# Moving the starting addresses of the matmul operands in a hybrid decoder layer

## The chip, the cores and the metric

The kernel runs on one core of a Trainium2 chip. The metric is the device time of one execution in microseconds. The times of the kernel before come from three executions.

## What is computed

One decoder layer on x of 512 tokens by 2048 features, in float32, and a last norm. A conditioning vector c gives a shift, a scale and a gate for each of the two sub-layers. The first sub-layer runs eight heads of causal stick-breaking attention beside a gated linear recurrence (RG-LRU) and projects both together; the second is an MLP of width 8192 with a squared ReLU.

```python
mod = (silu(c) @ w_ada + b_ada).reshape(B, 6, D)
sh1, sc1, gt1, sh2, sc2, gt2 = mod[:, 0..5]
h = rmsnorm(x, g_norm_mix) * (1 + sc1) + sh1
q, k, v, xr, xg = split(h @ w_in)
o_attn = stick_breaking_attention(q, k, v)
o_lru = rg_lru(causal_depthwise_conv(xr)) * gelu(xg)
x = x + gt1 * (concat(rmsnorm(o_attn), rmsnorm(o_lru)) @ w_out)
h = rmsnorm(x, g_norm_mlp) * (1 + sc2) + sh2
x = x + gt2 * (square(relu(h @ w_mlp_in)) @ w_mlp_out)
return rmsnorm(x, g_norm_final)
```

## The kernel before

**How the products are made.** Features lie on the 128 partitions, tokens along the free axis. Nearly every product is made from two halves of each float32 number: a high part, rounded to the type float32r, and a low part, the difference. Three matmuls then make one product: weights high by operand high, weights high by operand low, weights low by operand high (`mm3`, lines 251 to 256, and by hand at lines 463 to 465 for v and 1092 to 1094 in the MLP). So every matmul reads two buffers of the on-chip memory (SBUF): 128 columns of weights, which a separate instruction loads (PEld in the profile), and 256 or 512 columns of the moving operand. For the product that makes v, the roles are exchanged: there `a` is loaded as weights and `wh`, `wl` move.

**The buffers.** A tile of a name (a "tag") takes one of a few buffers in turn. Those that matmuls read:

- `a`: 64 buffers of 512 columns, the activations and their halves (and, in the first stage, the weights too); `n` and `cb`, small work and the conditioning row; the constants `ones`, `ntri`, `nones_r` of 128 columns each.
- `wr` (weights as loaded), `wh` and `wl` (their halves), 512 columns, up to the MLP. After it the same memory holds `w3` (768 columns) and `w5` (1024).
- `x` and `tt`, 1024 and 1280 columns, for the conditioning weights and for attention. After it the same memory holds `ts`, `raw` and `w4` (1024 columns).

The memory of a partition is filled from both ends. On the left stand the small constants, then `cb`, `n`, `a`, `ga`, then the stage's weights (lines 48 to 57, 79 to 91 and 131 to 138). On the right, downward from the top, stand the other buffers of the stage. `vec` begins at byte 16,512, which is 128 past a multiple of 512; the right side begins at byte 229,344, 480 past one. A tile takes whole units of 32 bytes. The buffers of matmul operands are multiples of 512 bytes long, so one number says where all of a side begin, counted from a multiple of 512 bytes:

| buffers | before |
|---|---|
| `ones`, `ntri`, `nones_r`, `cmask` | 0 |
| `cb`, `n`, `a` | 192 |
| `wr`, `wh`, `wl`; later `w3`, `w5` | 320 |
| `x`, `tt`; later `ts`, `raw`, `w4` | 480 |

**The order of the work.** The first stage (to about 110 us) makes the recurrence's input from `a` by `a` with all eight banks of the accumulator memory, while the conditioning weights stream in through VectorE (`prep1`, lines 370 to 377, and the loop at 409). Then come q, k and v (`qk_group`, `v_group`, `group`), with attention and the recurrence as generators between them (`Lane`, lines 262 to 296, gives each a number of ticks), the gate xg and the output projection (`product`, `half_product`). From about 750 us the MLP runs as a Strassen scheme of seven products of 256 columns for each pair of blocks (`strassen`, lines 1073 to 1098; `operands`, 1043 to 1066). There `operands` splits weights as loaded into `w3`, and sums of them into a high and a low tile that come from four `w4` and one `w5` in turn (`split_tag`, line 81). VectorE forms the sums (L1050, L1057, L1058) and the low halves (L121), ScalarE the high halves. The last 1024 features of the MLP go in plain products, and the last norm ends the kernel.

Small constants: `mods` (96 columns, the six modulation vectors), `gm1` and `gm2` (16, norm gain by scale), `spl`, `nspl`, `spe`, `shb` (8, 8, 8, 16, for the recurrence), `eps`. They are read as scalars of one column.

Of the kernel before, what the change touches and what calls it, by code (L numbers as in the profile page):

```python
# [10 lines left out]
F32 = mybir.dt.float32  # L11
# [5 lines left out]
P = 128  # L17
S = 512
D = 2048
NK = D // P  # L20
HEADS = 8
# [19 lines left out]

URGENT = 150
EVAC = 88

# [17 lines left out]
def hybrid_layer_kernel(  # L64
# [12 lines left out]
):  # L77
    nc = tc.nc
    sp = ctx.enter_context(tc.tile_pool(name="sp", bufs=1))
    region = {side: ctx.enter_context(ExitStack()) for side in ("right", "left")}  # L80
    pools, split_tag = {}, itertools.cycle(["w4"] * 4 + ["w5"])

    def stage(name):
        side, tags = STAGES[name]
        for tag in [t for t, (_, _, s) in pools.items() if s == side]:
            del pools[tag]
        region[side].close()
        pool = region[side].enter_context(tc.tile_pool(name=name, bufs=1, reuse_waits="tile", side=side))
        for tag, bufs in tags.items():
            pools[tag] = pool, bufs, side  # L90
            new(tag)
# [5 lines left out]
    def T(tag, dt=F32, cols=None):  # L97
        return new(next(split_tag) if tag == "w4" else tag, dt, cols)

    def new(tag, dt=F32, cols=None):  # L100
        count[0] += 1
        pool, bufs = (sp, BUFS[tag]) if tag in BUFS else pools[tag][:2]
        return pool.tile([P, cols or COLS[tag]], dt, tag=tag, name=f"{tag}_{count[0]}", bufs=bufs)
# [5 lines left out]
    def const(cols, name, dt=F32):  # L109
        return sp.tile([P, cols], dt, tag=name, name=name)  # L110
# [19 lines left out]

    vec = const(NPK, "vec")
    ones, ntri, nones_r = const(P, "ones"), const(P, "ntri", F32R), const(P, "nones_r", F32R)
    cmask, eps, mods = const(P, "cmask"), const(1, "eps"), const(96, "mods")
    gm1, gm2 = const(NK, "gm1"), const(NK, "gm2")
    spl, nspl, spe, shb = const(HEADS, "spl"), const(HEADS, "nspl"), const(HEADS, "spe"), const(2 * HEADS, "shb")
    cb = [T("cb"), T("cb")]
    stage("rows")
    stage("front")
    nc.scalar.dma_start(vec, pk)
# [122 lines left out]
    class Lane:  # L262
# [8 lines left out]
        def next(self):  # L271
            if not self.queue:
                return False
            try:
                self.wait += next(self.queue[0]) or 0.0
            except StopIteration:
                self.queue.pop(0)
            return True
# [155 lines left out]
    for o in range(8):  # L434
        t = T("a")
# [11 lines left out]
    def qk_evac(bs, h0, os=range(4)):  # L447
        for b in os:
            h, lo = T("a", F32R), T("a", F32R)
            s = QSCALE if b < 2 else 1.0  # L450
            with tc.high_priority(offset=EVAC):
                act(h, bs[b], AF.Copy, scale=s)
# [14 lines left out]
    def v_evac(bs, h0, os=range(4)):  # L467

        for o in os:
            p, b = o // 2, o % 2  # L470
            h, lo = T("a", F32R), T("a", F32R)
            with tc.high_priority(offset=EVAC):
                act(h, bs[o], AF.Copy)
# [140 lines left out]
    def scores(hd):  # L614
# [18 lines left out]
        nh, nl = T("tt", F32R), T("tt", F32R)  # L633
        with tc.high_priority(offset=EVAC):
            act(nh, e, AF.Copy)
# [605 lines left out]
    for i, (n, ps) in enumerate(parts):  # L1241
        seen = {m for m, _ in parts[: i + 1]}
        left = [m for m, _ in parts[i + 1 :]]
# [11 lines left out]
        if n not in left and n < NO - 1:  # L1255
# [10 lines left out]
            with tc.high_priority(offset=SETW):  # L1266
                for k, tok, q in quarters(n, *qs):
                    t = x2[k][:, tok]
# [8 lines left out]
        else:  # L1277
            with tc.high_priority(offset=SETE):
                for j, b in enumerate(bs):
                    t = T("a")  # L1280
# [14 lines left out]
    for p in final:  # L1295
        t = T("a", F32R)
# [156 lines left out]
```

## Time and profile before

| what | value |
|---|---|
| time, median of 3 | 2045.92 us (2044.84 to 2047.92) |
| span of the profiled execution, first to last instruction | 2043.4 us |
| share of the span in the chain that ended last: TensorE | 55% |
| the same: VectorE, DMA, issue | 3%, 1%, 1% |
| DMA moved | 441.45 MB, 216 GB/s mean |

No time of its own besides the span is given for the profiled execution; the span is 2.5 us under the median of the executions without a profile. A matmul in the profile has a start and a duration, but matmuls are pipelined and overlap: of 128x256 ones, 282 ns long by the profile, one starts every 119 ns or so. So the durations say little, and the time between starts is the quantity to read. "MATMUL ps_mm<-a,w 128*128 128x256" is a matmul into a bank of the pool `mm`, with moving operand or weights in `a` and in a tile whose name begins with w.

### The profile page before, as it was taken

How to read it: one execution, taken by the hardware profiler on the slowest of the kernel's cores; microseconds unless marked ns; L12 is line 12 of the kernel's file. 1: busy time of each engine (PE TensorE's matmuls, PEld its weight loads, DVE VectorE, ACT ScalarE, POOL GpSimd, SP SyncE). 2: the span in 40 equal slices, each digit the busy share in tenths (PEclk: the TensorE clock that was granted, in tenths of full speed). 3: DMA queues.
4: the chain of work that ended last, by engine and by line, in shares of the span. 5: the costliest groups of instructions: out<-in, count | busy, mean ns of one | idle time of the engine just before them, and what ended most of it. 6: DMA issues, size and time to landing. Idle time of an engine off the chain costs nothing.

```text
span 2043.4 us, 37927 instructions
## 1 busy us (share of the span) xinstructions
PE 2003.8 (98%) x14532; PEld 1890.2 (93%) x14532; DVE 1764.1 (86%) x2971; ACT 1078.3 (53%) x1572; POOL 180.7 (9%) x283
## 2 busy tenths in 40 slices
PE   8999999999999998999999999999999999999997
PEld 6788898778788998999999999999999999999996
DVE  8998776988898599999999999999778778778986
ACT  5443664796433485655555555456445445545542
POOL 0000000000000001121112112200010110210000
PEclk9999999999999999999999999999999999999998
DMA  9895645556689454676556556655476667667644
GB/s 364 299 326 195 214 150 187 177 171 208 219 277 338 145 153 157 190 231 206 195 194 221 193 174 221 227 190 182 150 281 226 230 237 249 228 242 254 243 149 150
DMA packets 205624, 441.45 MB, mean 216 GB/s; under 512 B 20353, under 2 KB 41985, under 8 KB 205442
## 3 DMA queue, kind: packets, MB, share of 16 engines
q1 hardware_dynamic: 178642, 360.78, 52.9%
q0 software_dynamic: 21760, 71.32, 9.4%
q10 hardware_dynamic: 5040, 6.93, 1.0%
q8 instruction: 114, 1.87, 0.4%
q14 instruction: 68, 0.56, 0.1%
HBM read 375.25 MB, written 63.70 MB: 215 GB/s over the span
## 4 chain that ended last, share of the span: by engine, by line
PE 55%; DVE 3%; DMA 1%; issue 1%; ACT 0%; SPq 0%; DVEq 0%; ACTq 0%
PE ps_mm L1093 9%; PE ps_mm L1094 9%; PE ps_mm L1092 9%; PE ps_z L1093 7%; PE ps_z L1094 7%; PE ps_z L1092 7%; PE ps_o L1094 2%; PE ps_o L1093 2%; PE ps_o L1092 2%; DVE w L121 1%; DMA raw<-in_w_mlp_out_dram 1%; DMA a<-x 0%; DMA a<-sum 0%; DVE a L1269 0%; DVE a L1339 0%
## 5 line engine op out<-in xcount | busy, mean ns | idle before, releaser
L1094 PE MATMUL ps_mm<-a,w 128*128 128x256 f32 x1696 | 477.3, 282 | 1.3 <-DVE w L121 1.3
L1093 PE MATMUL ps_mm<-a,w 128*128 128x256 f32 x1696 | 478.5, 282 | 0.0
L1092 PE MATMUL ps_mm<-a,w 128*128 128x256 f32 x1696 | 474.9, 281 | 0.0
L1056 ACT ACTIVATE w<-raw 128x768 fp32r<-128x768 f32 x244 | 204.9, 841 | 349.5 <-PE ps_mm L1093 158.8
L121 DVE TENSOR_TENSOR w<-ts,w 128x1024 fp32r<-128x1024 f32 x244 | 298.0, 1221 | 101.2 <-PE ps_mm L1093 52.9
L1094 PE MATMUL ps_z<-a,w 128*128 128x256 f32 x1304 | 368.3, 283 | 6.2 <-DVE w L121 6.2
L1093 PE MATMUL ps_z<-a,w 128*128 128x256 f32 x1304 | 368.4, 283 | 0.0
L1092 PE MATMUL ps_z<-a,w 128*128 128x256 f32 x1304 | 366.4, 281 | 0.0
L1062 ACT ACTIVATE w<-ts 128x1024 fp32r<-128x1024 f32 x244 | 258.5, 1059 | 129.5 <-DVE ts L1058 117.4
L1094 PEld LDWEIGHTS ps_mm<-a,w 128*128 128x128 f32 x1696 | 319.3, 188 | 1.6 <-DVE w L121 1.5
L1092 PEld LDWEIGHTS ps_mm<-a,w 128*128 128x128 f32 x1696 | 319.8, 189 | 0.1
L1093 PEld LDWEIGHTS ps_mm<-a,w 128*128 128x128 f32 x1696 | 319.0, 188 | 0.3 <-DVE a L121 0.2
L121 DVE TENSOR_TENSOR w<-raw,w 128x768 fp32r<-128x768 f32 (+1 forms) x296 | 267.3, 904 | 36.8 <-ACT w L237 24.9
L1094 PEld LDWEIGHTS ps_z<-a,w 128*128 128x128 f32 x1304 | 246.2, 189 | 7.3 <-DVE w L121 7.1
L1092 PEld LDWEIGHTS ps_z<-a,w 128*128 128x128 f32 x1304 | 246.6, 189 | 0.2
L1093 PEld LDWEIGHTS ps_z<-a,w 128*128 128x128 f32 x1304 | 245.8, 189 | 0.2
L237 ACT ACTIVATE wh<-wr 128x512 fp32r<-128x512 f32 (+1 forms) x184 | 113.2, 619 | 162.5 <-PE ps_mm L255 67.8
L252 PE MATMUL ps_mm<-a,wh 128*128 128x512 f32 x448 | 178.1, 397 | 1.5 <-DVE a L453 0.9
L256 PE MATMUL ps_mm<-a,wl 128*128 128x512 f32 x448 | 177.6, 396 | 0.5 <-DVE wl L121 0.4
L255 PE MATMUL ps_mm<-a,wh 128*128 128x512 f32 x448 | 176.8, 395 | 0.0
L1050 DVE TENSOR_TENSOR ts<-raw 128x512 f32<-128x512 f32 x244 | 166.6, 684 | 8.0 <-DMA raw<-in_w_mlp_out_dram 7.8
L121 DVE TENSOR_TENSOR wl<-wr,wh 128x512 fp32r<-128x512 f32 (+1 forms) x184 | 123.4, 674 | 35.8 <-ACT wh L237 35.1
(332 smaller groups left out, 4152.2 us busy)
## 6 DMA issues: line engine op xcount, KB each, us to landing
raw<-in_w_mlp_out_dram SPq DMA_DIRECT2D x124, 512.0 KB, 4.2
raw<-in_w_mlp_in_dram SPq DMA_DIRECT2D x120, 512.0 KB, 3.8
x<-in_w_adaT_dram SPq DMA_DIRECT2D x108, 512.0 KB, 5.9
wr<-in_w_in_dram SPq DMA_DIRECT2D x160, 256.0 KB, 3.4
tt<-in_w_adaT_dram SPq DMA_DIRECT2D x52, 512.0 KB, 6.6
part<-a POOLq DMA_DIRECT2D x84, 256.0 KB, 3.7
a<-part SPq DMA_DIRECT2D x84, 256.0 KB, 6.3
prod<-a POOLq DMA_DIRECT2D x63, 256.0 KB, 5.9
```

The lines of the kernel that those rows point to most:

```text
L121: tt(out=out, in0=full, in1=f32(high), op=ALU.subtract)
L237: act(h[:, :n], r[:, :n], AF.Copy)
L252: first = mm(out, wh, ah, start=start, stop=False, **kw)
L255: mm(out, wh, al, start=False, stop=False, **kw)
L256: mm(out, wl, ah, start=False, stop=stop, **kw)
L1050: tt(out=t[:, : 2 * HT].rearrange("p (a b) -> p a b", a=2), in0=r[:, HT : 3 * HT].rearrange("p (a b) -> p a b", a=2), in1=r[:, q_(0)].unsq ...
L1056: act(h, r[:, HT:], AF.Copy)
L1062: act(h, t, AF.Copy)
L1092: mm(out, wh[:, blk(i)], ah, start=st, stop=False, **kw)
L1093: mm(out, wh[:, blk(i)], al, start=False, stop=False, **kw)
L1094: mm(out, wl[:, blk(i)], ah, start=False, stop=j == js[-1], **kw)
```

## The change

The buffers are placed anew; nothing else is edited.

- Three small constants, `mods`, `gm1` and `spl`, move to a pool of their own at the top of the right side, ahead of everything there. They take 384 + 64 + 32 = 480 bytes.
- On the left remain `eps`, `gm2`, `nspl`, `spe` and `shb`, 32 + 64 + 32 + 32 + 64 = 224 bytes, after `cmask`. `ga` (4 buffers of 32 bytes) now follows them, and then a constant `pad` of 40 columns, 160 bytes, that nothing reads or writes.
- `new(...)` is called once for `ga`, `n` and `a` only to fix the order in which the pool places them. The tiles that it makes are not used.
- The stack of pools of the two sides (`region`) is opened after the new pool instead of at the start.

By this arithmetic `cb`, `n`, `a` and the stage's weights begin at 224 + 128 + 160 = 512, a multiple, and so do the buffers of the right side, 480 below a place 480 past one. In the MLP the left side then ends at byte 192,000, where the right side begins.

```diff
+PAD = 40
...
     sp = ctx.enter_context(tc.tile_pool(name="sp", bufs=1))
-    region = {side: ctx.enter_context(ExitStack()) for side in ("right", "left")}
+    region = {}
...
     ones, ntri, nones_r = const(P, "ones"), const(P, "ntri", F32R), const(P, "nones_r", F32R)
-    cmask, eps, mods = const(P, "cmask"), const(1, "eps"), const(96, "mods")
-    gm1, gm2 = const(NK, "gm1"), const(NK, "gm2")
-    spl, nspl, spe, shb = const(HEADS, "spl"), const(HEADS, "nspl"), const(HEADS, "spe"), const(2 * HEADS, "shb")
+    top = ctx.enter_context(tc.tile_pool(name="top", bufs=1, side="right"))
+    cmask, eps, gm2 = const(P, "cmask"), const(1, "eps"), const(NK, "gm2")
+    nspl, spe, shb = const(HEADS, "nspl"), const(HEADS, "spe"), const(2 * HEADS, "shb")
+    mods, gm1, spl = (top.tile([P, n], F32, tag=t, name=t) for n, t in ((96, "mods"), (NK, "gm1"), (HEADS, "spl")))
+    region |= {side: ctx.enter_context(ExitStack()) for side in ("right", "left")}
+    new("ga")
+    const(PAD, "pad")
     cb = [T("cb"), T("cb")]
+    for tag in ("n", "a"):
+        new(tag)
     stage("rows")
     stage("front")
```

## The prediction

> **What bounds the kernel now.** I read the page first, then the table of busy time by stage, then the waits of TensorE, and last the timeline of single matmuls.
>
> ```profile
> span 2043.4 us, 37927 instructions
> PE 2003.8 (98%) x14532; PEld 1890.2 (93%) x14532; DVE 1764.1 (86%) x2971; ACT 1078.3 (53%) x1572; POOL 180.7 (9%) x283
> ```
>
> TensorE is busy for 98% of the span, VectorE for 86%. In the table by stage the columns are the stretch, its length, busy time and instructions of PE, PEld, DVE, ACT and POOL, the granted clock, the DMA share and GB/s:
>
> ```profile
> 0.00:110.00 110.00, 98.00 (x399) 77.32 (x400) 100.08 (x192) 52.22 (x85) 5.25 (x9) 0.98 0.92 335
> 110.00:700.00 590.00, 584.93 (x3101) 497.49 (x3100) 475.55 (x808) 307.00 (x479) 14.46 (x14) 1.00 0.66 218
> 700.00:800.00 100.00, 93.22 (x749) 91.86 (x748) 88.86 (x188) 70.01 (x142) 3.52 (x6) 0.97 0.40 125
> 800.00:1000.00 200.00, 199.35 (x1676) 198.88 (x1674) 196.44 (x340) 108.98 (x145) 37.50 (x55) 1.00 0.66 214
> 1000.00:1400.00 400.00, 399.98 (x3367) 399.55 (x3366) 381.01 (x645) 218.00 (x292) 59.33 (x87) 1.00 0.61 202
> 1400.00:1990.00 590.00, 588.40 (x4944) 587.33 (x4944) 486.30 (x728) 307.13 (x404) 60.62 (x112) 1.00 0.63 224
> 1990.00:2043.40 53.40, 39.96 (x310) 37.76 (x308) 35.83 (x76) 14.98 (x31) 0.00 (x0) 0.90 0.45 147
> ```
>
> From 110 to 1990 us TensorE hardly stops, at the full granted clock. The longest waits of TensorE are these (who waited, for whom: total us, times, longest):
>
> ```profile
> PE ps_mm L252 <- ACT a L375: 7.7, 2, 5.2
> PE ps_z L1094 <- DVE w L121: 6.2, 3, 4.1
> ```
>
> So nothing is to be won by removing waits. The time is the number of matmuls times the spacing of their starts, and the change can act only through that spacing. VectorE stands close behind: 196.44 of 200 us from 800 to 1000, and 381.01 of 400 up to 1400.
>
> The spacing is what I looked at next. The first stage multiplies `a` by `a`: moving operand and weights both begin 192 bytes past a multiple of 512. Start (us), duration, engine, line:
>
> ```profile
> 66.94 0.39 PE L252 MATMUL ps_z<-a,a 128*128 128x512 f32 x1
> ...
> 74.42 0.39 PE L252 MATMUL ps_o<-a,a 128*128 128x512 f32 x1
> ```
>
> From the first to the last lie eleven output blocks of three matmuls, 33 spacings in 7.48 us: 226.7 ns for 512 columns. In the projections the moving `a` stands at 192 and the weights `wh`, `wl` at 320:
>
> ```profile
> 520.22 0.39 PE L256 MATMUL ps_z<-a,wl 128*128 128x512 f32 x1
> ...
> 529.32 0.40 PE L256 MATMUL ps_z<-a,wl 128*128 128x512 f32 x1
> ```
>
> 13 blocks, 39 spacings in 9.10 us: 233.3 ns, for the same shape and the same order of three matmuls per block. The slower case has the higher mean clock (1.00 against 0.98) and the lighter load on memory (DMA share 0.66 against 0.92). What differs is where the weights begin. In the MLP (`a` at 192, `w3` and `w5` at 320, `w4` at 480) the row of 1000 to 1400 us gives 400.00 / 3367 = 118.8 ns for 256 columns. Two steps of 42 matmuls each there, from the first L1092 of one to that of the next:
>
> ```profile
> 1279.51 0.28 PE L1092 MATMUL ps_mm<-a,w 128*128 128x256 f32 x1
> ...
> 1284.55 0.28 PE L1092 MATMUL ps_mm<-a,w 128*128 128x256 f32 x1
> ...
> 1289.55 0.28 PE L1092 MATMUL ps_mm<-a,w 128*128 128x256 f32 x1
> ...
> 1294.51 0.28 PE L1092 MATMUL ps_mm<-a,w 128*128 128x256 f32 x1
> ```
>
> The first takes 5.04 us (120.0 ns each) and, by the order of the tiles in the code, has its high sum weights in `w4` and its low ones in `w5`; the second takes 4.96 us (118.1 ns) and has both in `w4`. Nothing waits in either. So the mixture of starting positions moves the spacing by 1.6% inside one stage.
>
> One more view says why the weights' position can matter. Loads of weights (PEld) and matmuls:
>
> ```profile
> 1279.39 0.19 PEld L1092 LDWEIGHTS ps_mm<-a,w 128*128 128x128 f32 x1
> 1279.51 0.19 PEld L1093 LDWEIGHTS ps_mm<-a,w 128*128 128x128 f32 x1
> ...
> 67.17 0.19 PEld L256 LDWEIGHTS ps_z<-a,a 128*128 128x128 f32 x1
> 67.17 0.39 PE L255 MATMUL ps_z<-a,a 128*128 128x512 f32 x1
> ```
>
> The load of the next weights starts with the running matmul (both at 1279.51, both at 67.17), with 512 columns as with 256: two streams leave the same memory at the same moment. In the first stage they begin at the same place of a 512-byte block and the matmul keeps 226.7; in the projections and the MLP they begin at different places.
>
> **The change, part by part.** By the sizes in the code, with every small tile taking a multiple of 32 bytes, the left side had 704 bytes of small constants ahead of `cb`, `n`, `a` (512 + 192), and `ga` put another 128 ahead of the weights (320). The right side began 32 bytes short of a multiple (480). After: 224 bytes of constants, 128 of `ga` and 160 empty make 512; `mods`, `gm1` and `spl` take 480 on the right. Everything that matmuls read begins at 0. The two sides then meet with no byte between them in the MLP.
>
> No instruction, DMA or wait is added or removed, and none changes its engine or queue, so the queues of SP, ACT and POOL keep their contents and order. The moved constants (`mods`, `gm1`, `spl`) are read as one-column scalars by the same instructions: nothing, by their unchanged count. The extra tiles that fix the order of the pools are never written: nothing.
>
> What is priced is the spacing. Its value with all bases equal and 256 columns is not in the trace. Above it lies the dear step, 120.0 ns; below it the pace of the loads themselves, which shows where 128-column matmuls run:
>
> ```profile
> 202.05 0.19 PEld L255 LDWEIGHTS ps_z<-a,a 128*128 128x128 f32 x1
> 202.16 0.19 PEld L256 LDWEIGHTS ps_z<-a,a 128*128 128x128 f32 x1
> 202.27 0.19 PEld L252 LDWEIGHTS ps_z<-a,a 128*128 128x128 f32 x1
> 202.38 0.19 PEld L255 LDWEIGHTS ps_z<-a,a 128*128 128x128 f32 x1
> ```
>
> That is 110 ns. Between 110 and 120.0 I take 113.4, half of 226.7: the first 256 columns of the first stage run under the same simultaneous load of 128 columns, and equal bases are what both share. Saving against 118.8: 5.4 ns. With 512 columns I take the row itself, 226.7: 233.3 - 226.7 = 6.6 ns.
>
> [...]
>
> Counts from 110 to 700 us:
>
> ```profile
> L252 PE MATMUL ps_mm<-a,wh 128*128 128x512 f32 x445 | 176.9, 397 | 1.5 <-DVE a L453 0.9 <-DVE a L474 0.6
> L252 PE MATMUL ps_z<-a,wh 128*128 128x512 f32 x96 | 38.0, 396 | 0.0
> L463 PE MATMUL ps_mm<-wh,a 128*128 128x256 f32 x128 | 36.3, 284 | 0.4 <-DVE a L453 0.4
> ```
>
> Each L252 has an L255 and an L256 with it, so 3 x 541 = 1623 matmuls here, and some 150 more on the other banks (attention's own, with changing widths, left out): 1770 x 6.6 = 11.7 us. L463 to L465 and the first halves of the output projection are some 960 of 256 columns: 960 x 5.4 = 5.2 us. Together 16.9; I take 14, since VectorE is at 81% and stops cost more than their length. After one in the first stage the spacing is out of step for a while:
>
> ```profile
> 64.30 0.50 PE L255 MATMUL ps_mm<-a,a 128*128 128x512 f32 x1 [1.03 <-DVE a L376]
> 64.64 0.39 PE L256 MATMUL ps_mm<-a,a 128*128 128x512 f32 x1
> ```
>
> From 64.64 to 66.94 ten matmuls take 2.30 us, 230 each, and then the 226.7 is back. Attention's short matmuls make such breaks too.
>
>
> 700 to 800 us: some 700 x 5.4 = 3.8, of which I take 2: VectorE has 88.86 us of work there and TensorE already idles 6.8.
> 800 to 1000: 1676 x 5.4 = 9.1, but VectorE's 196.44 us remain and become what is late next: 2.
> 1000 to 1400: 3367 x 5.4 = 18.2. TensorE would need 381.8, VectorE 381.01; two engines that meet do not both run full. If VectorE keeps the 98.2% that it reaches from 800 to 1000, 388 us: 12. I take 13.
> 1400 to 1990: 4944 x 5.4 = 26.7; VectorE's 486 us fit in 563. Stops at the ends of products stay: 25.
> After 1990: 310 matmuls, 1.
> The first 110 us keep their spacing (bases equal before and after): 0. DMA is at 0.92 there, and a new start of its rows in memory has no row to price it; VectorE's 100.08 us bound a gain at 10, and a loss of 10 would be as much again. I take 0, the value of equal bytes in equal packets.
>
> Sum: 14 + 2 + 2 + 13 + 25 + 1 = 57 us. Span 2043.4 - 57 = 1986.4. The median without profiling, 2045.92, is 2.5 above this span, and I carry that over: **1989 us**. With no loss to VectorE it would be 76 us and 1970; if a third of the matmuls fail to settle, 2008.
>
> **Rivals.**
>
> Only the wide matmuls gain. With 256 columns the load of weights (110 ns) fills nearly the whole matmul (113.4), so the two streams may never come clear of each other; with 512 there is free time in the second half. Then 110 to 700 us gives some 10: 2036; a half effect lies between. For it: the spacing per column is already higher with 256 columns (118.8 against 233.3 / 2 = 116.7). Against it: the first half of a wide matmul has the same overlap and shows no loss at 226.7. Chance 0.14.
>
> Nothing happens: 226.7 belongs to the first stage for another reason (weights and operand out of one pool), or the empty tile is dropped and the bases are not what the code intends. For it: attention's scores also have both operands in `a`, yet their three wide ones start at 200.82, 201.05 and 201.28, 230 ns apart:
>
> ```profile
> 200.82 0.40 PE L252 MATMUL ps_z<-a,a 128*128 128x512 f32 x1
> 201.05 0.39 PE L255 MATMUL ps_z<-a,a 128*128 128x512 f32 x1
> 201.28 0.39 PE L256 MATMUL ps_z<-a,a 128*128 128x512 f32 x1
> ```
>
> Against it: three matmuls are fewer than the ten that it took above to settle, and the two MLP steps differ by positions alone. 2046, chance 0.16.
>
> Slower: with equal bases both streams ask for the same part of the memory in step, and where the load has no slack (the 256-column products from 700 to 1990 us, TensorE-bound) every matmul pays for it. If all take the 120.0 ns of the dear step, 10,700 x 1.2 = 13 us: 2059; the dearest single spacing of the first step would be the far end:
>
> ```profile
> 1280.46 0.29 PE L1094 MATMUL ps_mm<-a,w 128*128 128x256 f32 x1
> 1280.59 0.28 PE L1092 MATMUL ps_mm<-a,w 128*128 128x256 f32 x1
> ```
>
> That is 130 ns, 11.2 above the mean: 2166 if all took it; I hold the mean of the step nearer. It decides as soon as the mean there exceeds 118.8. Against it stands the first stage, where equal bases go with the best spacing. Chance 0.12.
>
> Better still: a start at 0 touches fewer blocks than one at 192, and the loads' 110 ns become the bound. Saving 8.8 ns: 40 us after 1400, 15 from 800 to 1400 (VectorE's limit), some 27 before 700, 5 elsewhere: 87 us, 1959. No row shows it. Chance 0.06.
>
> **How the numbers follow.** The forecast has 0.52, with a range of its own from 1970 to 2008. A difference of 0.2%, 4 us, is about what a measurement of this kernel can tell. Faster: 0.52 + 0.14 + 0.06 = 0.72; within 0.2%: 0.16; slower: 0.12. The range from 1966 to 2049 takes in the forecast with a few us of the first stage, the narrow gain and no change (to the upper run of before and a little), and leaves out the slower case and the best one.
>
> **What would show it.** Right: the MLP's matmuls start 113 to 114 ns apart after 1400 us, in a steady beat instead of one that goes up to 130; the wide ones of the projections 226.7; the first stage is as before; VectorE at 98% or more from 800 to 1400, with new waits of L1094 for `w`. Wrong: equal spacing in all stages (no effect), a gain before 700 us alone (the loads decide), or a spacing over 118.8 in the MLP.

## The result and the profile after

| | before | after |
|---|---|---|
| median, us (11 executions each) | 2045.58 (2044.14 to 2047.92) | 2050.55 (2048.01 to 2054.55) |
| span of the profiled execution, us | 2043.4 | 2050.1 |

The ratio is 1.0027, with a 95% interval from 1.0018 to 1.0035: the change makes the kernel slower by some 5 us, where 57 us less were forecast. Of the kernel `split` below and of the kernel before in its session, one execution each took 6.9 ms; the medians and ratios are those of the others. In what follows, most lines of the code after stand 7 lower than before (L1092 is L1099, L252 is L259, but L121 is L122); the kernels of the experiments shift them by a few lines more.

The head of the page after, and the table by stage (stretch, its length, busy time and instructions of PE, PEld, DVE, ACT and POOL, granted clock, DMA share, GB/s):

```profile
span 2050.1 us, 37927 instructions
...
PE 2009.6 (98%) x14532; PEld 1904.8 (93%) x14532; DVE 1764.0 (86%) x2971; ACT 1077.8 (53%) x1572; POOL 181.0 (9%) x283
```

```profile
0.00:110.00 110.00, 98.16 (x401) 77.58 (x402) 100.35 (x192) 51.89 (x86) 5.59 (x9) 0.98 0.92 337
110.00:700.00 590.00, 582.96 (x3138) 503.68 (x3137) 478.32 (x815) 308.52 (x483) 14.46 (x14) 1.00 0.67 218
700.00:800.00 100.00, 94.47 (x763) 93.31 (x762) 91.76 (x190) 71.05 (x140) 5.77 (x10) 0.98 0.42 131
800.00:1000.00 200.00, 199.00 (x1655) 198.56 (x1654) 194.35 (x336) 107.73 (x141) 37.23 (x55) 1.00 0.66 216
1000.00:1400.00 400.00, 400.00 (x3331) 399.67 (x3330) 376.43 (x638) 216.09 (x289) 57.30 (x84) 1.00 0.61 198
1400.00:1990.00 590.00, 588.50 (x4896) 587.70 (x4895) 482.59 (x722) 304.74 (x401) 60.64 (x112) 1.00 0.64 223
1990.00:2050.10 60.10, 46.51 (x362) 44.29 (x360) 40.21 (x83) 17.79 (x34) 0.00 (x0) 0.91 0.41 138
```

The instructions are the same in number and kind, and the clock and the DMA share hardly differ. What differs is how many matmuls fit in each stretch. Counted from the start, the kernel after leads by 39 matmuls at 700 us (3539 against 3500) and by 53 at 800; it leads by 32 at 1000, is 4 behind at 1400 and 52 behind at 1990. At 120 ns each, 52 matmuls are 6.2 of the 6.7 us by which its span is longer. So the change gains before the MLP and loses more inside it.

Single matmuls show why. First stage of the kernel after, and its projections (start, duration, engine, line):

```profile
66.86 0.39 PE L259 MATMUL ps_z<-a,a 128*128 128x512 f32 x1
...
74.34 0.39 PE L259 MATMUL ps_o<-a,a 128*128 128x512 f32 x1
```

```profile
515.03 0.39 PE L259 MATMUL ps_z<-a,wh 128*128 128x512 f32 x1
...
518.43 0.39 PE L259 MATMUL ps_o<-a,wh 128*128 128x512 f32 x1
```

In the first stage 33 spacings take 7.48 us, 226.7 ns each, as before. In the projections 15 spacings take 3.40 us: also 226.7, where 233.3 stood before. Then the MLP of the kernel after:

```profile
1300.03 0.28 PE L1100 MATMUL ps_mm<-a,w 128*128 128x256 f32 x1
1300.15 0.28 PE L1101 MATMUL ps_mm<-a,w 128*128 128x256 f32 x1
1300.27 0.28 PE L1099 MATMUL ps_mm<-a,w 128*128 128x256 f32 x1
...
1305.91 0.28 PE L1101 MATMUL ps_mm<-a,w 128*128 128x256 f32 x1
```

49 spacings in 5.88 us: 120.0 ns, the same all through. The beat is as steady as forecast, but it is the dear step's beat, above the 118.8 of before.

TensorE's longest waits after are those of before, with one small new one among them, for `wh` from ScalarE (L244), and one that grew from 0.9 to 1.1 us (L460, before L453) (who waited, for whom: total, times, longest):

```profile
PE ps_mm L259 <- ACT a L382: 7.6, 2, 5.4
PE ps_z L1101 <- DVE w L122: 6.2, 4, 4.1
...
PE ps_mm L259 <- ACT wh L244: 1.4, 2, 0.9
...
PE ps_mm L259 <- DVE a L460: 1.1, 2, 0.8
```

### The profile page after: what moved, and what is told of

Read it like the earlier page. It is cut to its first block, busy times and chain, and to the rows that moved or that the text cites. A ratio compares the mean times of both kernels' runs of the same rounds, so it can differ in the third digit from the quotient of the medians.

```text
span 2050.1 us, 37927 instructions
## 1 busy us (share of the span) xinstructions
PE 2009.6 (98%) x14532; PEld 1904.8 (93%) x14532; DVE 1764.0 (86%) x2971; ACT 1077.8 (53%) x1572; POOL 181.0 (9%) x283
## 4 chain that ended last, share of the span: by engine, by line
PE 57%; DVE 2%; DMA 1%; issue 0%; ACT 0%; SPq 0%; DVEq 0%
PE ps_mm L1101 9%; PE ps_mm L1100 9%; PE ps_mm L1099 9%; PE ps_z L1101 7%; PE ps_z L1100 7%; PE ps_z L1099 7%; PE ps_o L1101 2%; PE ps_o L1099 2%; PE ps_o L1100 2%; DMA raw<-in_w_mlp_out_dram 1%; DMA a<-x 0%; DVE w L122 0%; DMA a<-sum 0%; DVE a L1346 0%; DVE a L1276 0%
## 5 line engine op out<-in xcount | busy, mean ns | idle before, releaser
L1099 PE MATMUL ps_mm<-a,w 128*128 128x256 f32 x1696 | 479.2, 283 | 0.0
L122 DVE TENSOR_TENSOR w<-ts,w 128x1024 fp32r<-128x1024 f32 x244 | 298.0, 1221 | 116.9 <-PE ps_mm L1100 61.6
L1099 PE MATMUL ps_z<-a,w 128*128 128x256 f32 x1304 | 369.3, 284 | 0.0
L1101 PEld LDWEIGHTS ps_mm<-a,w 128*128 128x128 f32 x1696 | 325.5, 192 | 1.4 <-DVE w L122 1.4
L1100 PEld LDWEIGHTS ps_mm<-a,w 128*128 128x128 f32 x1696 | 325.7, 192 | 0.2 <-DVE a L122 0.2
L1099 PEld LDWEIGHTS ps_mm<-a,w 128*128 128x128 f32 x1696 | 325.5, 192 | 0.1
L1069 ACT ACTIVATE w<-ts 128x1024 fp32r<-128x1024 f32 x244 | 258.2, 1058 | 113.4 <-DVE ts L1065 101.9
L122 DVE TENSOR_TENSOR w<-raw,w 128x768 fp32r<-128x768 f32 (+1 forms) x296 | 267.4, 904 | 34.3 <-ACT w L244 23.4
L1101 PEld LDWEIGHTS ps_z<-a,w 128*128 128x128 f32 x1304 | 250.6, 192 | 7.1 <-DVE w L122 7.0
L1099 PEld LDWEIGHTS ps_z<-a,w 128*128 128x128 f32 x1304 | 250.8, 192 | 0.1
L1100 PEld LDWEIGHTS ps_z<-a,w 128*128 128x128 f32 x1304 | 250.7, 192 | 0.1
L244 ACT ACTIVATE wh<-wr 128x512 fp32r<-128x512 f32 (+1 forms) x184 | 113.0, 618 | 152.2 <-PE ps_mm L262 65.8
L259 PE MATMUL ps_mm<-a,wh 128*128 128x512 f32 x448 | 176.2, 393 | 3.1 <-ACT wh L244 1.4
L122 DVE TENSOR_TENSOR wl<-wr,wh 128x512 fp32r<-128x512 f32 (+1 forms) x184 | 123.7, 675 | 33.3 <-ACT wh L244 32.8
```

The lines of the kernel that those rows point to most:

```text
L122: tt(out=out, in0=full, in1=f32(high), op=ALU.subtract)
L244: act(h[:, :n], r[:, :n], AF.Copy)
L259: first = mm(out, wh, ah, start=start, stop=False, **kw)
L1069: act(h, t, AF.Copy)
L1099: mm(out, wh[:, blk(i)], ah, start=st, stop=False, **kw)
L1100: mm(out, wh[:, blk(i)], al, start=False, stop=False, **kw)
```

## The experiments

**Theories.** T1: with equal starts, every matmul and its load of weights pay a fixed 13.3 ns above the bare columns, whatever the width: 512 columns take 226.7 and 256 take 120.0, so 256 columns more cost 106.7 ns, and both leave 13.3. What counts is the distance between the two starts. Two widths alone cannot prove such a division: the same two numbers also read as 113.3 for each 256 columns, as the prediction had it, and 6.7 more for a narrow matmul, whose load, 110 ns by the rows in the prediction, fills it nearly whole (T1b). Rivals of both: T2, it is the multiple of 512 that costs or gains, not the equality; T3, the cost goes by the column, and the MLP's 120.0 has another cause (its buffers, its order); T4, any uniform starts give a steady beat, and the loss comes from elsewhere.

In what follows the distance is the start of the weights less the start of `a`, modulo 256 bytes. The kernels of the first two groups differ from the one after only in the constants that stand ahead of `cb` (`low_`), behind `a` (`mid_`) and at the top of the right side (`top_`), and in the empty bytes behind them.

**Equal starts at another place, and a distance of 256.** The first puts `a` and all weights at byte 192 of 512, the second `a` at 0 and all weights at 256.

```diff
+    low_, mid_, top_ = ('mods', 'gm1', 'gm2', 'shb'), (), ('eps', 'spl', 'nspl', 'spe')
```

> All bases equal again, but 192 bytes past a multiple of 512 instead of on one. If the distance between the weights' base and the moving operand's base decides, everything is as in the changed kernel: one start every 120.0 ns with 256 columns, every 226.7 with 512, time 2050.5. If it is the multiple of 512 as such that costs, the 256-column matmuls go back to 118.8 and the time to about 2035 if the wide ones keep 226.7, to 2045.6 if they don't.

```diff
+    low_, mid_, top_ = ('mods',), ('gm1', 'gm2', 'shb', 'eps', 'spl'), ('nspl', 'spe')
```

> All weights 256 bytes, half of a 512-byte block, past the moving operands. If the distance counts within 512 bytes, the two streams are as far apart as they can be and the 256-column spacing should be the lowest of these four, below 118 (110 is the pace of the loads), time below 2040. If it counts within 256 bytes, this is the same as equal bases: 120.0, 226.7 and 2050.5.

Measured: 2051.8 (ratio to before 1.0028, 1.0019 to 1.0038) and 2049.28 (1.0014, 1.0005 to 1.0024). Both have the beats of the kernel after, 120.1 in the MLP on average and 229.0 to 229.1 for the wide matmuls. T2 falls: a multiple of 512 is worth nothing by itself. A distance of 256 bytes acts as one of 0; that the distance counts modulo 256 elsewhere too is taken from this one pair.

**Other distances.** `a` at 0, all weights at one distance from it: the lines are those for 32, 64, 96, 128, 192 and 224 bytes.

```diff
+    low_, mid_, top_ = ('mods',), ('eps',), ('gm1', 'gm2', 'shb', 'spl', 'nspl', 'spe')
+    low_, mid_, top_ = ('mods',), ('gm1',), ('gm2', 'shb', 'eps', 'spl', 'nspl', 'spe')
+    low_, mid_, top_ = ('mods',), ('gm1', 'eps'), ('gm2', 'shb', 'spl', 'nspl', 'spe')
+    low_, mid_, top_ = ('mods',), ('gm1', 'gm2'), ('shb', 'eps', 'spl', 'nspl', 'spe')
+    low_, mid_, top_ = ('mods',), ('gm1', 'gm2', 'shb'), ('eps', 'spl', 'nspl', 'spe')
+    low_, mid_, top_ = ('mods',), ('gm1', 'gm2', 'shb', 'eps'), ('spl', 'nspl', 'spe')
```

> Weights 32 bytes past the moving operands. If places within a block of 64 bytes are alike, this is as equal bases: 120.0 and 226.7, time 2050. If each 32 bytes count, the value lies between those of 0 and 64: a fast beat of 113.3 for some stretches or the 118.4 that the w4 tiles had before at 288 (32 within 256), time 2020 to 2046.

> Moving operands begin at 0, all weights 64 bytes further on. If the distance decides, the beat of equal bases is gone: the spacing with 256 columns is another than 120.0 (118 to 119 as before, or better) and with 512 columns 230 to 233. If it is enough that all bases of a kind are uniform, 120.0 and 226.7 stay and the time is 2050.5.

> Weights 96 bytes past the moving operands. If places within a block of 64 bytes are alike, this is as 64: 113.3 or 117.8, time 2009 to 2035. If each 32 bytes count, it lies between 64 and 128 (118.8): time 2030 to 2044.

> All weights 128 bytes past the moving operands: the distance that the kernel before had between its activations and the left side, now for the right side too. If the distance decides: the repeating 115, 118, 122, 120, 119 of before everywhere, mean 118.8, wide ones 232.6, time 2044 to 2047. If uniform bases are enough for the fixed beat: 120.0 and 226.7, 2050.5.

> Weights 192 bytes past the moving operands, which within 256 bytes is 64 behind them. If the distance counts without its sign, this is as 64: starts 113.3 ns apart where the fast beat holds, 117.8 elsewhere, time 2009 to 2035. If the sign counts, because the moving stream is the faster and either runs away from the weights or catches up with them, the fast beat of 64 is missing here and the time is 2040 to 2051.

> Weights 224 bytes past the moving operands, 32 behind within 256 bytes. Without a sign, as the kernel with 32. With a sign, as 192. If neither, the two streams have no rule that counts distance alone, and the absolute place of the weights within 64 bytes would have to enter.

Measured (spacings in ns from the starts of one profiled execution: the MLP's between 1400 and 1890 us, differences over 240 left out; the projections' wide ones and v's, differences over twice the usual left out; for v the roles are exchanged, so its distance is the negative one):

| distance | median, us | ratio to before | MLP | wide | v |
|---|---|---|---|---|---|
| mixed (before) | 2045.58 | 1 | 118.8 | 234.2 | 119.4 |
| 0 (after) | 2050.55 | 1.0027 (1.0018 to 1.0035) | 120.1 | 229.0 | 120.2 |
| 32 | 2041.21 | 0.9979 (0.9969 to 0.9988) | 118.5 | 234.5 | 117.1 |
| 64 | 2026.74 | 0.9892 (0.9840 to 0.9943) | 113.5 | 234.4 | 118.1 |
| 96 | 2040.97 | 0.9977 (0.9961 to 0.9994) | 118.8 | 235.4 | 120.0 |
| 128 | 2043.53 | 0.9989 (0.9980 to 0.9999) | 118.8 | 234.1 | 119.4 |
| 192 | 2031.55 | 0.9927 (0.9912 to 0.9942) | 117.9 | 231.0 | 115.3 |
| 224 | 2031.70 | 0.9932 (0.9917 to 0.9947) | 117.9 | 234.7 | 118.9 |

T4 falls: at 128 all starts are uniform, the MLP's mean is 118.8 and not 120.1, and the time is within 0.2% of before. The distance sets the spacing, and the one that the change chose has the best value for 512 columns and the worst for 256. The order differs between the widths, so one width's best distance can't be read from the other's.

At distance 64 the same code has two beats. From its trace, two places of the MLP:

```profile
1100.05 0.28 PE L1104 MATMUL ps_mm<-a,w 128*128 128x256 f32 x1
...
1102.77 0.28 PE L1104 MATMUL ps_z<-a,w 128*128 128x256 f32 x1
...
1299.89 0.28 PE L1104 MATMUL ps_z<-a,w 128*128 128x256 f32 x1
...
1302.95 0.28 PE L1103 MATMUL ps_mm<-a,w 128*128 128x256 f32 x1
```

24 spacings in 2.72 us are 113.3 ns; 26 in 3.06 us are 117.7. The beat of 113.3 held for the most part from 902 to 1248 us and from 1405 to 1890, the other one for the most part between. That profiled execution took 2008.65 us, the least of four; others took up to 2034.97, which would fit a different share of the two beats, but they have no trace. So the row of 64 in the table sets a spacing from the fastest execution beside the median of all four. The changes of beat in this trace come at irregular spacings: one of 142 ns at 901.4 us, and at 1248 us two of 797 and 532 ns, where TensorE waits 0.52 and 0.25 us for VectorE. Other stops, of 475 ns at 1095 us and of 865 at 1171, leave the beat as it was. What chooses between the two stays open. The short beat is not that of 64 alone: at distance 192 it held from 897 to 928 us.

**One part of the change at a time.** The first is the kernel before with 384 empty bytes ahead of the projections' weights, which puts these at 192, where `a` is, and leaves the MLP as it was. The second is the kernel after with 128 empty bytes there, which takes the equality from the projections and leaves it to the MLP.

```diff
-    "front": ("left", {"wr": 4, "wh": 3, "wl": 3}),
+    "front": ("left", {"pf": 1, "wr": 4, "wh": 3, "wl": 3}),
```

> The kernel before, with an empty tile of 384 bytes ahead of the weights of the projections alone, so that they begin where the activations do (192); the MLP's tiles stay where they were. By the distance theory, only the 512-column matmuls change, from 232.6 to 226.7: 1770 x 5.9 = 10.4 us less, and v's 768 of 256 columns go from 119.4 to 120.3: 0.7 more. Time 2035 to 2036, MLP as before at 118.7. If the gain in the changed kernel's projections came from the multiple of 512, nothing moves: 2045.

> The changed kernel, with an empty tile of 128 bytes ahead of the weights of the projections, so that these stand 128 past the activations as in the kernel before; all tiles of the MLP stay at multiples of 512. By the distance theory this leaves only the loss: the MLP at 120.0, some 10,900 x 1.5 = 16 us, less what stops hide: 2059 to 2062. If equal bases cost nothing in the MLP and the loss lies elsewhere, 2045.

Measured: 2041.57 (0.9982, 0.9973 to 0.9991) and 2055.21 (1.0048, 1.0033 to 1.0063), beside 2045.26 for before: 3.7 us less and 10.0 more. Together that is 6.3 more, against 5.0 for the whole change, so the two parts nearly add. Both are smaller than expected. The first one's table by stage shows what became of the gain:

```profile
110.00:700.00 590.00, 583.79 (x3154) 503.65 (x3153) 478.27 (x816) 309.25 (x485) 14.49 (x14) 1.00 0.67 219
700.00:800.00 100.00, 93.43 (x752) 91.82 (x751) 92.25 (x191) 70.15 (x140) 6.23 (x10) 0.97 0.43 130
800.00:1000.00 200.00, 198.75 (x1666) 197.94 (x1666) 195.45 (x341) 108.27 (x142) 36.88 (x54) 1.00 0.68 216
```

With 403 matmuls before 110 us it has done 3557 at 700 us, 57 more than the kernel before: a lead of 6.8 us at 119 ns. From 800 to 1000 us, where VectorE is busy for 195.45 us, ten of the 57 are lost again (1666 against 1676). The wide matmuls reach 229.2 on average and not 226.7: 1355 of their 1664 spacings there are 226 or 227 ns, and most of the others 231 to 237. That stops put them out of step, as the one in the first stage did, is a reading of this.

**Width alone.** In the kernel after, 384 of the projections' products issue each 512-column matmul as two of 256 columns, with the same buffers and the same equal starts.

```diff
...
+            for i, (w, v) in enumerate(((wh, ah), (wh, al), (wl, ah))):
+                for p in (0, 1):
+                    c = slice(p * 256, p * 256 + 256)
+                    m = mm(out[:, c], w, v[:, c], start=start and i == 0 and p == 0, stop=stop and i == 2 and p == 1, **kw)
...
```

> The changed kernel, but 1152 of the 512-column matmuls of the projections are issued as two of 256 columns each, with the same weights loaded twice and the same equal starts. If equal starts cost a fixed 13.3 ns for each matmul and its load, whatever the width, a pair takes 2 x 120.0 = 240.0 instead of 226.7: 1152 x 13.3 = 15 us more, 2066, and the timeline of the projections shows a beat of 120.0. If the cost goes by the column, as the prediction had it (113.4 is half of 226.7), a pair takes 226.7, the time stays at 2050 to 2052, and the 120.0 of the MLP has another cause (its buffers or its order).

Measured: 2066.97 (median of three executions; 1.0116, 1.0096 to 1.0137). Its timeline of the projections, where a row stands for 2 or 4 matmuls:

```profile
520.17 0.64 PE L264 MATMUL ps_z<-a,wh 128*128 128x256 f32 x4
520.65 0.40 PE L264 MATMUL ps_z<-a,wl 128*128 128x256 f32 x2
520.89 0.64 PE L264 MATMUL ps_z<-a,wh 128*128 128x256 f32 x4
521.37 0.40 PE L264 MATMUL ps_z<-a,wl 128*128 128x256 f32 x2
521.61 0.64 PE L264 MATMUL ps_z<-a,wh 128*128 128x256 f32 x4
```

Six matmuls take 0.72 us: 120.0 ns each, 240 for a pair that as one matmul takes 226.7. T3 falls: same buffers, same stage, same starts, and two narrow matmuls take 13.3 ns more than one wide one of as many columns. 1152 x 13.3 ns = 15.4 us would make 2066; the median is 16.4 above that of the kernel after. T1 gives this, the fixed cost coming a second time with the second matmul, and so does T1b, with 6.7 for each of the two.

**Length of the load.** In the kernel after, two of each three matmuls of the Strassen products load 64 columns of weights instead of 128.

```diff
...
-                    mm(out, wh[:, blk(i)], al, start=False, stop=False, **kw)
-                    mm(out, wl[:, blk(i)], ah, start=False, stop=j == js[-1], **kw)
+                    c = slice(i * P, i * P + 64)
+                    mm(out[:64], wh[:, c], al, start=False, stop=False, **kw)
+                    mm(out[:64], wl[:, c], ah, start=False, stop=j == js[-1], **kw)
```

> The changed kernel, but in the Strassen products of the MLP the second and third matmul of each three (weights high by operand low, weights low by operand high) load 64 columns of weights instead of 128, with equal starts as before. So the corrections for half of the output's rows are left out. If the cost of equal starts comes of the load filling the whole matmul, as the slower rival said, it shrinks with the load: half the cost for two loads of three gives spacings of 113 to 116 on average, and 2010 to 2025. If it is a fixed 32 cycles for each load, the beat stays at 120.0 and the time at 2050.

Measured: 2019.6 (0.9884, 0.9848 to 0.9920). Its MLP:

```profile
1499.77 0.28 PE L1099 MATMUL ps_o<-a,w 128*128 128x256 f32 x1
1499.88 0.28 PE L1101 MATMUL ps_o<-a,w 128*64 128x256 f32 x1
1500.00 0.28 PE L1102 MATMUL ps_o<-a,w 128*64 128x256 f32 x1
...
1502.43 0.28 PE L1102 MATMUL ps_z<-a,w 128*64 128x256 f32 x1
```

23 spacings in 2.66 us: 115.7 ns instead of 120.0, with the same moving columns. If the 13.3 ns go by the length of the load, loads of 128, 64 and 64 columns cost 13.3 + 6.7 + 6.7, 8.9 on average, and 106.7 + 8.9 = 115.6. By T1b, 120.0 for the one full load and 113.3 for each of the two short ones make 115.6 as well. So the beat is shorter with the shorter loads, and this run doesn't tell the two readings apart. Nor does either give the single spacings, which are 117, 117 and 113 ns in turn. The edit also halves the rows of output that these matmuls write, and no run separates that from the load. The 32 cycles of the expectation come to 13.3 ns only if a cycle is what a column takes in T1, 106.7 / 256 = 0.417 ns; no run shows the length of a cycle. The mean over 1400 to 1890 us is 116.3; the beat is less regular there.

**Combinations.** Three kernels keep `a` at 0 and set the projections' and the MLP's weights apart with an empty first tile (`pm`, `pf`) in the pools of the MLP, the projections or both: projections equal and MLP at 64; projections equal and MLP at 224; projections at 192 and MLP at 64. The line is that of `pm`:

```diff
...
-    "mlp": ("left", {"w5": 1, "w3": 6}),
+    "mlp": ("left", {"pm": 1, "w5": 1, "w3": 6}),
...
```

> The two best distances together: the projections' weights at the base of the activations (226.7), the MLP's weights 64 bytes past it. The wide matmuls give 10 to 13 us against the kernel with 64 everywhere: 1996 to 2024, and as wide a scatter, since the 256-column matmuls have two beats there, 113.3 and 117.8, and a stop decides which one follows. If the wide matmuls' beat does not carry into the later stages, the two gains add up: 2045.1 - 9.7 - 37 (all at 113.3, less VectorE's part) is the lowest to be had, near 1996.

> The projections' weights at the base of the activations, the MLP's weights 224 bytes past it. With 224 everywhere the MLP ran at 116.6 and the four timed runs lay within 1.5 us; the wide ones stood at 234.5. Now they take 226.7: 1770 x 7.8 = 14 us less, v's 0.9 more: 2018 to 2020, steady.

> The best combination so far (projections' weights equal to the operand, MLP's weights 64 bytes ahead: 2022.6) with the projections' weights 192 bytes ahead instead of equal. The product that makes v, which loads the operand as weights, then sees a distance of 64 bytes and took 113 to 115 ns there instead of 120: 768 x 5 to 6 = 4 us less; the wide ones take 229 to 231, as much as the equal ones on average (229). 2017 to 2020 if distance alone decides and the two parts add; 2022 to 2027 if the MLP keeps the slower of its two beats (117.8) longer.

| projections, MLP | median, us | ratio to before | MLP | wide | v |
|---|---|---|---|---|---|
| 0, 64 | 2022.60 | 0.9889 (0.9876 to 0.9903) | 117.7 | 229.1 | 120.2 |
| 0, 224 | 2027.86 | 0.9910 (0.9895 to 0.9925) | 117.9 | 228.9 | 120.3 |
| 192, 64 | 2022.78 | 0.9894 (0.9863 to 0.9925) | 117.8 | 231.0 | 117.2 |

The projections take the spacing of their own distance and the MLP that of its own: 229 beside 117.7. The second came out 8 us over what was expected of it. The third came out where it was expected if the MLP keeps the slower of its two beats, but v, at a distance of 64, took 117.2 and not the 115.3 that it had at the same starts with all weights at 192, and the wide ones paid 2 ns, so nothing was won over the first. At distance 64 the shorter beat can't be counted on. All three are about 1% faster than both kernels of this case.

## Why the prediction was wrong

**What held.** The change acts through the spacing of the matmuls: equal counts (37927 instructions), equal clock (0.995), no new wait over 1.5 us. Wide matmuls settle at 226.7 ns with equal starts, in the first stage and in the projections, and the beat becomes steady. The first 110 us kept their pace (401 matmuls against 399).

**The step that failed** is "Between 110 and 120.0 I take 113.4, half of 226.7: the first 256 columns of the first stage run under the same simultaneous load of 128 columns, and equal bases are what both share." It gave a whole narrow matmul the pace of half a wide one. Half the columns do not make half the load: each narrow matmul has a load of 128 columns to itself, and with equal starts it takes 120.0 ns, in the MLP and in the projections of `split` alike, 6.7 more than that half. With shorter loads it falls to 115.7. Whether a fixed 13.3 comes with every matmul (106.7 + 13.3) or 6.7 with a narrow one alone (113.3 + 6.7) stays open. Of the terms of the sum, those of the MLP, 2 + 2 + 13 + 25, and the 1 after 1990 us rest on this step, and so do 5.2 of the 16.9 us before 700. In its place the narrow matmuls lost: 10.0 us in the kernel that has equal starts in the MLP alone.

**The term of 14 us before 700 us** was right in mechanism for the wide matmuls and too large: the lead of 39 matmuls at 700 us is 4.7 us. The wide ones reach 229.0 on average and not 226.7 (5.2 x 1728 = 9.0 us where 11.7 stood); v's spacing rose from 119.4 to 120.2 instead of falling by 5.4 (0.6 lost where 5.2 was to be won); and TensorE was busy for 582.96 us of this stretch instead of 584.93, 2.0 of idling more. These three make 6.4; what took the other 1.7 is not accounted for.

**VectorE's ceiling** was about the right size, though the change never met it. At distance 64 the stretch from 1000 to 1400 us has this row:

```profile
1000.00:1400.00 400.00, 398.30 (x3450) 396.72 (x3449) 392.16 (x664) 224.21 (x301) 57.95 (x85) 1.00 0.62 205
```

VectorE is busy for 98.0% of it (the prediction assumed 98.2%), and the 83 matmuls more than before are 9.9 us, where 13 stood. The row mixes the two beats; in its part from 1000 to 1250 us, nearly all at 113.3, VectorE is busy for 245.3 of 250 us, 98.1%, and at 1248 us TensorE waits for it, 0.52 and 0.25 us.

**The rivals.** The slower one had the direction and the price, 120.0, right. Its reason, a load without slack that every narrow matmul pays for, is T1b, one of the two readings that the runs leave. It left out what the wide matmuls gain, so its 2059 lies 8 above the result; the kernel with equal starts in the MLP alone took 2055.21. "Only the wide matmuls gain" named the same reason, the load that fills a narrow matmul, but took it for no change where it is a loss. The argument against it, that the first half of a wide matmul shows no loss at 226.7, was the failed step again: a loss that comes with the matmul, or with a load that fills it, does not show there. "Better still" needed 110 ns; the lowest steady beat for 256 columns in any run here is 113.3, at distance 64. Its reason, the start at 0, fell with T2: with all starts at 192 the MLP has the same 120.1.

**What stays open:** why the spacing depends on the distance as it does, what chooses the beat at 64, and which of T1 and T1b holds; a run with shorter loads for wide matmuls would tell these two apart. That both streams meet in the same part of the memory was argued and not shown; shown are the dependence on the distance, on the number of matmuls and, with the reservation above, on the length of the load.

## What to carry to other kernels

Before you carry a spacing to another width, ask what part of it comes by the column and what part by the matmul: half of a wide matmul's 226.7 ns was not the time of a narrow one here, 120.0. Two widths don't settle the division. The one that fits equal starts fits no other distance of the table: 256 columns more cost 106.7 ns there, but by the means 234.1 - 118.8 = 115.3 at 128 and 234.4 - 113.5 = 120.9 at 64. So measure each width at each distance. In this kernel, where TensorE is busy for 98% of the span and the 14532 matmuls come with 14532 loads of weights, trying out the distance was worth about 1%, at the cost of an empty tile. Equal starts are good for wide matmuls here (226.7 ns against 233.3) and bad for narrow ones (120.0 against 118.8).

## What had not been expected of the hardware

- Setting the weights 64 or 192 bytes off the moving operand is worth 0.7 to 1.1% of this kernel; the spacing of 256-column matmuls goes from 120.0 (distances 0 and 256) to 113.3 (64).
- The sign of the distance matters: 32 took 2041.21 us and 224, which is 32 the other way, 2031.70. Between 64 and 192 the wide matmuls differ, 234.4 against 231.0 ns; in the MLP both have the beats of 113.3 and 117.8, and the intervals of their times overlap.
- One and the same code runs at 113.3 or at 117.7 ns, for a hundred microseconds and more at a stretch. At distance 64 the beat changed at the stops at 1248 us (spacings of 797 and 532 ns) and not at those at 1095 and 1171; from 1000 to 1400 us TensorE was busy for 398.30 of 400 us.
